# Seven block products for the down projections of two feed-forward blocks, with sums made by DMA

## The chip, the cores and the metric

The kernel runs on one core of one Trainium2 chip. The metric is device time in microseconds of one execution; the time before is the median of three runs.

## The reference

Three transformer-like blocks run one after the other on a sequence of 1024 tokens with 1024 features, all in float32. What matters here is the feed-forward part of each block, and in the second block a convolution:

```python
# first_block: D_FF = 4096 (called f1 in the kernel)
h = h + jnp.square(jax.nn.relu(hn @ w_up[layer])) @ w_down[layer]
...
# second_block: D_FF_2 = 2816 (f2), and a causal depthwise convolution of 31 taps on 256 channels
yc = causal_dwconv(yc, conv_w[l], conv_b[l])
...
hidden = jax.nn.silu(u[..., :D_FF_2]) * u[..., D_FF_2:]
x = x + jnp.einsum('bsf,fd->bsd', hidden, w_down[l])
...
# third_block: D_FF_3 = 4096 (f3)
f = jnp.square(jax.nn.relu(h @ w_fc1)) @ w_fc2
x = x + gate2 * rms_norm_3(f, norm2_post)
```

## The kernel before

Activations lie feature-major: a tile of 128 features by 1024 tokens, or by a half of 512. Every float32 operand of a big product is split into a rounded part and a remainder (`split`: ScalarE copies to the high part, L319, VectorE subtracts for the low part, L305), and every 128x128 by 128x512 product is three matmuls (`mm3`). So all weights, and all activations that return from DRAM, cost a 512 KB load, one ScalarE and one VectorE pass of 1024 columns.

`Stream` (`W`) is the list of all operands ("units") in the order of their use. A unit is loaded by the SyncE (SP) DMA queue into a `raw` buffer (two of them, four during a feed-forward block), and split into one of four slots of ring A, or two of ring B, as soon as one is free. `tick` is called after each group of matmuls and makes at most one split; `nd < ns + 2` keeps the loads at most two units ahead of the splits. `k.pe` counts the TensorE time of the matmuls written so far; it is a count made while the program is written, not a clock of the chip.

`up7` computes hidden = relu(x @ up)^2 with seven block products in place of eight (the pieces t1, t2, t3, t4 of the activations are made once; sums of weight halves are made by VectorE). It has groups of two units of 128 features: the first 8 (f1, f2) or 12 (f3) groups have one product computed ahead and reload it (`start`, a DMA of the GpSimd queue). Each hidden piece of 128x512 goes to DRAM (`gd`). `down7` reads them back, four units at a time, and makes the plain product with the down weights: for each 128x512 output tile, four units by three matmuls, and VectorE adds the tile to the residual in `X`. For f3 the last four units are done in parts of 512, 256 and 256 tokens, so that the last norm is short. `ada` units (weights of a small product, made by VectorE) are put between those of f1 and f2.

The residual of f1 and f2 is loaded into `X` by the GpSimd queue (`load_half`) before the first add. For f3 the residual is read back by the SP queue (`take_slots`, and one 2 MB load in `tail`).

In block 2 the convolution is spread over the first projections: VectorE does 18 of the 31 taps per channel block, ScalarE 12, GpSimd adds the ScalarE products into `cb` (`self.tt(cb, cb, s, ALU.add, nc.gpsimd)`).

Background work (norms, the convolution, the gated attention) is written as generators that `step` and `fine` advance between matmuls; each engine runs its instructions in the order in which they were written.

Of the kernel before, what the change touches and what calls it, by code (L numbers as in the profile page):

```python
# [8 lines left out]
F32 = mybir.dt.float32  # L9
# [47 lines left out]


def _feat(a):

    return np.ascontiguousarray(a.T.reshape(KT, P, a.shape[0]).transpose(1, 0, 2))


def lay_out(i):
# [16 lines left out]
    a["w1_up"] = _cols(i["w_up"][0])  # L81
    a["w1_down"] = i["w_down"][0].reshape(32, P, D)
    w = i["w_in_2"][0]
# [22 lines left out]
    a["w3_up"] = _cols(i["w_fc1_3"])  # L106
    a["w3_down"] = i["w_fc2_3"].reshape(32, P, D)

# [39 lines left out]
class Stream:  # L148
# [5 lines left out]
    def __init__(self, k):  # L154
        self.k = k
        self.seq = []
        self.nd = self.ns = 0
        self.free = {"A": 4, "B": 0}
        self.pools = {}
        self.bphase = ()  # L160
        self.raws = []
        self.groom = [False, False]

# [39 lines left out]
    def _split(self):  # L203
# [37 lines left out]
        self.ns += 1  # L241
        while self.nd < min(self.ns + 2, len(self.seq)):
            self.load()
        return True

    def tick(self):
        self.k.ada_flush()
        if self.ns < self.nd and self.k.pe - self.seq[self.ns].at > self.LEAD:
            self._split()
# [15 lines left out]
HALVES = ((0, 512), (512, 1024))  # L265


class Kern:
    def __init__(self, tc, a, out):
        self.tc, self.nc, self.a, self.out = tc, tc.nc, a, out  # L270
        self.bgs = []
        self.due = {}
        self.pe = 0.0
        self.clk = {tc.nc.vector: 0.0, tc.nc.scalar: 0.0, tc.nc.gpsimd: 0.0}
        self.stacks = []
        self.ada_pend = []
        self.adap = None


# [371 lines left out]

    CHUNKS = {"f1": [2, 2] + [4] * 7, "f2": [2] + [4] * 5, "f3": [2, 2] + [4] * 7}

# [4 lines left out]
    def setup(self):  # L658
# [46 lines left out]
        def ffn7(n, up, down, with_ada=0):  # L705
# [14 lines left out]
            for g in range(U):  # L720
# [3 lines left out]
                S[n + "g"].append(G)  # L724
            S[n + "h"], S[n + "d"] = [], []
            gd = S[n + "x"] = self.drp.tile([a[down].shape[0], P, T], F32, name="gd" + n)
            c = 0
# [167 lines left out]
    def up7(self, name):  # L895
# [10 lines left out]

        def relu2(dst, src, m, t, scale=1.0):
            self.act(dst, src, AF.Relu, scale=scale)
            self.act(dst, dst, AF.Square)
            nc.scalar.dma_start(out=gd[m, :, 512 * t:512 * t + 512], in_=dst)  # L910

# [11 lines left out]
        for g in range(0, M, 2):  # L923
# [7 lines left out]
            for i in (0, 1):  # L931
                u = first[g + i]
                self.part7(u, 512, H[1, 0], ps[i], False)
                W.done(u)
                s = scratch()
                if gated:
                    self.act(s, ps[i], AF.Copy)
                    nc.scalar.dma_start(out=cd[g + i], in_=s)
                else:
                    relu2(s, ps[i], 2 * (g + i), 0)  # L940
        self.wait(*self.norms.values())
# [6 lines left out]
        def slot():  # L948
            n[0] += 1
            return X1[:, (n[0] - 1) % 8]  # L950

# [5 lines left out]
        def start(g):  # L957

            ca = wide() if gated else None
            s1 = None  # L960
            if g < M:
                s1 = scratch() if gated else slot()
                nc.gpsimd.dma_start(out=s1, in_=sd[g])
                if gated:
                    nc.gpsimd.dma_start(out=ca[:, :512], in_=cd[g])
            return s1, ca

        if name == "f1":
            self.load_half(0)
        nxt = start(0)  # L970
        for g, G in enumerate(groups):
# [18 lines left out]
            if g >= M:  # L990
# [4 lines left out]
                else:  # L995
                    relu2(slot(), z, 2 * g, 0)
            x = self.ps()
# [10 lines left out]
            if not gated:  # L1008
                relu2(c22, c22, 2 * g + 1, 1)
            self.stt(c21, y, -1.0, w, ALU.mult, ALU.subtract)  # L1010
# [3 lines left out]
            else:  # L1014
                relu2(c21, c21, 2 * g + 1, 0)
            self.part7(W.get(d), 0, H[1, 1], x, False)
# [8 lines left out]
            else:  # L1025
                relu2(v, v, 2 * g, 1)
        W.groom[1] = True
        if name != "f3":
            for half in (0, 1)[name == "f1":]:
                self.load_half(half)  # L1030
        self.ext_es.close()
        self.open_ss()

    def load_half(self, half):
        c = half * 512
        for k in (0, 4):
            self.nc.gpsimd.dma_start(out=self.X[half][:, k:k + 4], in_=self.xd[:, k:k + 4, c:c + 512])

    def down7(self, name, add, tail, quarters=False):

        W = self.W
        D_, Gu = self.S[name + "d"], self.S[name + "h"]
        c = 0
        for j, n in enumerate(self.CHUNKS[name]):
# [9 lines left out]
            for part in self.PARTS if last and quarters else ((0, 0, 512), (1, 512, 1024)):  # L1054
                half, c0, c1 = part
                for m in range(KT):
# [12 lines left out]
                    while m == 0 and self.unsummed:  # L1069
                        self.fine(False, list(self.bgs))  # L1070
                    add(m, part, ps, first, last)
                    W.tick()
                    self.step()
# [27 lines left out]
    def add_ffn(self, a1, a2, g):  # L1101
        def add(m, part, ps, first, last):
            half, c0, c1 = part
            o = c0 - half * 512
            x = self.X[half][:, m, o:o + c1 - c0]
            self.tt(x, x, ps, ALU.add)
            if last:
# [44 lines left out]
    def block1(self):  # L1152
# [8 lines left out]
        dec = gp.tile([P, 2, 17], F32, name="dec")  # L1161
        lvl = gp.tile([P, 7, P], U8, name="lvl")
        g0, g0_es = self.pool("gate0", 1, None, "right")
        wg = g0.tile([NM, 256], F32, name="wg")
# [163 lines left out]
        for e in (gw_es, cp_es, tp_es, sg_es, gp_es):  # L1328
# [11 lines left out]
        self.up7("f1")  # L1340
        self.open_ring("f1d", ada=True)
        g = self.cols("norm_final_w")
        self.tt(self.g12, g, self.cols("ln1_g_2"), ALU.mult)
        a1, a2 = [], []
        self.down7("f1", self.add_ffn(a1, a2, g),
                 lambda part: self.norm2_gen(part, a1[part[0]], a2[part[0]], self.g12, None, g))
# [166 lines left out]
    def block2(self):  # L1513
# [18 lines left out]
        ca = [cp.tile([P, T], F32, name="ca%d" % m) for m in range(2)]  # L1532
        cb = cp.tile([P, T], F32, name="cb")

# [3 lines left out]

        NP = 12

        def conv():
            for m in range(2):
# [7 lines left out]
                self.ts(ca[m], yc[m][:, 0:T], w[0], self.col("conv_b_2", m), ALU.mult, ALU.add)  # L1550
                mul(1, cb)
                todo = list(range(2, 1 + NP))
                nd = 30 - NP
                for i, t in enumerate(range(1 + NP, 31)):
                    self.stt(ca[m], yc[m][:, t:t + T], w[t], ca[m], ALU.mult, ALU.add)
                    if todo and (NP - 1 - len(todo)) * nd <= i * (NP - 1):
# [7 lines left out]
                self.tt(ca[m], ca[m], cb, ALU.add)  # L1564
            for _ in range(5):
# [188 lines left out]


        self.up7("f2")
        self.open_ring("f2d", ada=True)
# [267 lines left out]
    def block3(self):  # L2025
# [203 lines left out]
        self.open_ring("f3d")  # L2229
        self.hp, e = self.pool("hp2", 1, None, "right")  # L2230
        self.ffn_es.insert(0, e)
        ac = []

        def add(m, part, ps, first, last):
            half, c0, c1 = part
            o = c0 - half * 512
            x = self.X[half][:, m, o:o + c1 - c0]
            if first:
                self.act(x, ps, AF.Copy)
            else:  # L2240
                self.tt(x, x, ps, ALU.add)
            if last:
                if m == 0 and o == 0:
                    ac.append(self.acc())
                if m == 0 and not xr:
                    take_slots()
                self.sq_add(ac[half], x, m, o)

        xr = []

        def take_slots():

            ts = []
            for q in "AB":
                while W.free[q] and len(ts) < 8:
                    W.free[q] -= 1
                    for n in ("hi", "lo"):
                        t = W.pools[q].tile([P, UW], F32R, tag=n, name="xr").bitcast(F32)[:, :T]
                        t = t.rearrange("p (a b) -> p a b", b=512)
                        k = len(ts)  # L2260
                        self.dma(t, self.xd[:, k:k + 2, 0:512])
                        ts.extend((t[:, 0], t[:, 1]))
            xr.append(ts)

        def tail(part):
            half, c0, c1 = part
            n, o = c1 - c0, c0 - half * 512
            self.unsummed = False
            if half and len(xr) < 2:
                t = self.hp.tile([P, KT, 512], F32, tag="h0", name="xr")  # L2270
                self.dma(t, self.xd[:, :, 512:])
                xr.append([t[:, k] for k in range(KT)])
            yield self.after(1.0)
# [6 lines left out]
            for k in range(KT + 1):  # L2280
# [3 lines left out]
                if k:  # L2284
                    f = self.X[half][:, k - 1, o:o + n]
                    x = xr[half][k - 1]
                    self.tt(f, f, x[:, o:o + n], ALU.add, gp if not half or k % 2 else None)
# [4 lines left out]
        self.down7("f3", add, tail, quarters=True)  # L2292

# [29 lines left out]
```

## Time and profile before

| what | us |
|---|---|
| median of 3 runs (3549.32 to 3553.84) | 3552.57 |
| the profiled execution, its own time | 3552.79 |
| its span, first to last instruction | 3550.7 |
| TensorE busy | 3421.8 |
| VectorE busy | 2258.7 |
| ScalarE busy | 1354.2 |
| GpSimd busy | 387.4 |

The mean granted TensorE clock is 0.978 of full speed. In the stages named here f1 lies at 500 to 1140 us of the span (down from 800), the convolution at 1230 to 1340, f2 at 1880 to 2520 (down from 2305), f3 at 2890 to 3534 (down from 3182).

### The profile page before, as it was taken

To read this page: it belongs to the slowest core of one execution; us is meant where nothing else is said; L and a number is where in the kernel's file an instruction comes from. 1 tells how busy PE (TensorE), PEld (TensorE's weight loads), DVE (VectorE), ACT (ScalarE), POOL (GpSimd) and SP (SyncE) were. 2 spreads that over 40 slices of the span, in tenths; PEclk is the share of its full clock that TensorE was granted. 3 is DMA by queue.
4 is the path that set the end of the run, shared out by engine and by line. 5 is a ranking of instruction groups with operands and counts; after the bars stand their busy time and mean duration, and the time that the engine had idled before them with its cause. 6 is when DMAs were issued, how large, how long until landed. Compare 5 with 4: busy or idle time off the path is not lost. (4 is left out here: it accounts for less than half of the span.)

```text
span 3550.7 us, 43690 instructions
## 1 busy us (share of the span) xinstructions
PE 3421.8 (96%) x16725; PEld 2813.7 (79%) x16725; DVE 2258.7 (64%) x3773; ACT 1354.2 (38%) x2018; POOL 387.4 (11%) x374
## 2 busy tenths in 40 slices
PE   7999999999999969999999999989999999999998
PEld 7788898888887757876698788778778878878887
DVE  5456376548665694567767988776665576645444
ACT  3432254442112442555634444421342564452111
POOL 0111020000001360000020000000132420000003
PEclk9999999999999979998999999999999999999999
DMA  3111444336443125445325322354222254443222
GB/s 106 48 43 48 151 138 165 115 117 207 145 137 101 62 82 172 133 123 153 85 105 165 122 84 85 108 206 140 89 76 63 82 182 149 134 163 119 95 83 72
DMA packets 176612, 413.07 MB, mean 116 GB/s; under 512 B 17832, under 2 KB 58488, under 8 KB 176276
## 3 DMA queue, kind: packets, MB, share of 16 engines
q1 hardware_dynamic: 133044, 325.34, 28.8%
q10 hardware_dynamic: 38304, 67.13, 5.1%
q0 software_dynamic: 5056, 17.83, 1.7%
q8 instruction: 131, 2.15, 0.3%
q14 instruction: 77, 0.63, 0.1%
HBM read 304.50 MB, written 105.63 MB: 116 GB/s over the span
## 5 line engine op out<-in xcount | busy, mean ns | idle before, releaser
L324 PE MATMUL mm<-Hh,whi 128*128 128x512 f32 (+3 forms) x3632 | 1384.7, 382 | 20.2 <-DVE X L305 12.0
L324 PE MATMUL mm<-Hl,whi 128*128 128x512 f32 (+3 forms) x3632 | 1370.2, 378 | 0.2
L324 PE MATMUL mm<-Hh,wlo 128*128 128x512 f32 (+3 forms) x3632 | 1366.1, 377 | 2.8 <-DVE wlo L305 2.8
L324 PEld LDWEIGHTS mm<-Hh,whi 128*128 128x128 f32 x3632 | 686.7, 189 | 162.1 <-DVE X L305 12.8
L324 PEld LDWEIGHTS mm<-Hh,wlo 128*128 128x128 f32 x3632 | 686.2, 189 | 136.0 <-DVE wlo L305 6.6
L324 PEld LDWEIGHTS mm<-Hl,whi 128*128 128x128 f32 x3632 | 686.9, 189 | 128.0 <-issue 1.2
L319 ACT ACTIVATE whi<-raw 128x1024 fp32r<-128x1024 f32 (+3 forms) x386 | 378.9, 992 | 711.2 <-PE mm L324 467.2
L305 DVE TENSOR_TENSOR wlo<-raw,whi 128x1024 fp32r<-128x1024 f32 (+3 forms) x386 | 451.2, 1176 | 178.9 <-ACT whi L319 166.3
L305 DVE TENSOR_TENSOR X<-X,mm 128x512 f32<-128x512 f32 (+1 forms) x478 | 312.2, 657 | 396.9 <-PE mm L324 389.8
L324 PE MATMUL mm<-t,whi 128*128 128x512 f32 x1296 | 408.6, 396 | 2.1 <-ACT whi L319 2.1
L324 PEld LDWEIGHTS mm<-t,whi 128*128 128x128 f32 x1296 | 243.0, 188 | 62.0 <-ACT whi L319 2.9
L324 PE MATMUL mm<-t,wlo 128*128 128x512 f32 x648 | 256.6, 396 | 2.2 <-DVE wlo L305 2.2
L319 ACT ACTIVATE Hh<-raw 128x1024 fp32r<-128x1024 f32 x86 | 89.3, 1057 | 381.5 <-PE mm L324 227.8
L321 ACT ACTIVATE X<-X 128x512 f32<-128x512 f32 (+1 forms) x226 | 151.9, 673 | 184.7 <-DVE X L310 152.8
L305 POOL TENSOR_TENSOR acc<-acc,sq 128x256 f32<-128x256 f32 (+1 forms) x108 | 116.2, 1077 | 912.2 <-ACT sq L321 836.9
L305 DVE TENSOR_TENSOR raw<-raw 128x512 f32<-128x512 f32 x216 | 145.2, 687 | 81.8 <-DMA raw<-in_w_up 79.8
L324 PEld LDWEIGHTS mm<-t,wlo 128*128 128x128 f32 x648 | 121.8, 188 | 33.5 <-DVE wlo L305 4.2
L305 DVE TENSOR_TENSOR Hl<-raw,Hh 128x1024 fp32r<-128x1024 f32 x86 | 104.5, 1221 | 45.6 <-ACT Hh L319 45.4
L324 PE MATMUL mm<-wlo,Hh 128*128 128x264 f32 (+4 forms) x336 | 111.5, 341 | 12.4 <-DVE wlo L305 12.4
L324 PE MATMUL mm<-whi,Hh 128*128 128x264 f32 (+4 forms) x336 | 112.0, 343 | 8.9 <-ACT whi L319 5.4
L310 DVE SCALAR_TENSOR_TENSOR ada<-raw,silc,ada 128x128 f32<-128x128 f32 x336 | 115.1, 350 | 7.9
L310 DVE SCALAR_TENSOR_TENSOR X<-mm,X 128x512 f32<-128x512 f32 x108 | 74.6, 690 | 60.3 <-PE mm L324 58.7
(290 smaller groups left out, 3467.8 us busy)
## 6 DMA issues: line engine op xcount, KB each, us to landing
raw<-in_w_up SPq DMA_DIRECT2D x136, 512.0 KB
raw<-gdf SPq DMA_DIRECT2D x86, 512.0 KB
raw<-in_w_down SPq DMA_DIRECT2D x86, 512.0 KB
gdf<-X ACTq DMA_DIRECT2D x108, 256.0 KB
raw<-in_w_ada SPq DMA_DIRECT2D x48, 512.0 KB
gdf<-X ACTq DMA_DIRECT2D x22, 512.0 KB
B<-qd SPq DMA_DIRECT2D x36, 256.0 KB
A<-qd SPq DMA_DIRECT2D x36, 256.0 KB
```

What stands on the lines that cost most here:

```text
L305: eng.tensor_tensor(out=out, in0=a, in1=b, op=op)
L310: self.nc.vector.scalar_tensor_tensor(out=out, in0=a, scalar=s, in1=b, op0=op0, op1=op1)
L319: self.nc.scalar.activation(out, in_, f, scale=scale, **kw)
L321: self.nc.scalar.activation(out, in_, f, bias=bias, scale=scale, **kw)
L324: self.nc.tensor.matmul(out, l, r, start=s, stop=e, skip_group_check=grp)
```

## The change

The down products of f1 and f3 are made in seven block products, each over all 16 pairs of hidden units: for the four quarters of a pair's weights (two units by two halves of the output features) and of its activations (two units by two halves of the tokens). Three products use a weight quarter as it is, four use a sum of quarters, called `sw`, which a list of DMAs makes in DRAM long before; the activation pieces are made by VectorE in `up7` and stored as seven pieces. Each product runs over eight e (two pairs each) with four PSUM tiles; both operands come through the stream, so each of the 56 steps of a down product needs two units of 512 KB. `sums` and `sums_step` issue 16 copies on the SP queue and 16 accumulating DMAs on the GpSimd queue for each of f1 and f3, one for each 12 us of `k.pe`: those of f1 in block 1, those of f3 from the start of f2's `up7`. `W.ahead` is 4 during the products.

For f1 all four residual loads are issued after `up7`. For f3 the residual is loaded into `Hh` by the GpSimd queue, and the last norm is one of 512 tokens. For f2 the first add becomes a ScalarE copy and the residual is added into `X` by four accumulating DMAs of 1 MB. In the convolution VectorE does 20 taps and ScalarE 10; the sums of the latter's products are made by accumulating DMAs of 512 KB in two tiles `cb`.

```diff
+def _quarters(w):
+    return np.ascontiguousarray(w.reshape(8, 2, 2, P, 2, 512).transpose(0, 2, 4, 3, 1, 5)).reshape(
+        8, 4, P, 2, 512)
...
-        while self.nd < min(self.ns + 2, len(self.seq)):
+        while self.nd < min(self.ns + self.ahead, len(self.seq)):
...
+    def sums(self, name, w):
+        S = self.S[name + "s"]
+        sync, pool = self.nc.sync, self.nc.gpsimd
+        for e in range(0, 8, 2):
+            r = slice(e, e + 2)
+            for i, q in ((0, 1), (2, 1), (1, 0), (3, 2)):
+                self.sums_todo.append((sync, S[i, r], w[r, q], {}))
+        for i, q in ((0, 3), (2, 0), (1, None), (3, None)):
+            for e in range(0, 8, 2):
+                r = slice(e, e + 2)
+                src = w[r, q] if q is not None else S[0 if i == 1 else 1, r]
+                self.sums_todo.append((pool, S[i, r], src, dict(accum_op=ALU.add, max_dma_last_dim=4096)))
+
+    def sums_step(self, pace=12.0):
+        if self.sums_todo and self.pe >= self.sums_at:
+            eng, dst, src, kw = self.sums_todo.pop(0)
+            eng.dma_start(out=dst, in_=src, **kw)
+            self.sums_at = self.pe + pace
...
+    ORDER = ("P1", "P2", "P6", "P7", "P4", "P5", "P3")
...
+                sw = S[n + "s"] = self.drp.tile([4, 8, P, 2, 512], F32, name="sw" + n)
+                A = {"P1": a[down][:, 0], "P2": a[down][:, 2], "P4": a[down][:, 3],
+                     "P5": sw[0], "P6": sw[1], "P7": sw[2], "P3": sw[3]}
+                for i in self.ORDER:
+                    for e in range(8):
+                        S[n + "d"].append([W.add(x[e].rearrange("p a b -> p (a b)"), D, n + "d")
+                                           for x in (A[i], gd[PIECE[i]])])
...
 (up7, at the end of each group, not for f2)
-                relu2(v, v, 2 * g, 1)
+                relu2(v, v)
+                t1_, t2_, t4_ = slot(), slot(), slot()
+                self.tt(t1_, ca, v, ALU.subtract)
+                self.tt(v, c22, v, ALU.subtract)
+                self.stt(t2_, t1_, -1.0, c22, ALU.mult, ALU.subtract)
+                self.stt(t4_, t2_, -1.0, c21, ALU.mult, ALU.subtract)
+                for i, t in ((3, t1_), (5, v), (4, t2_), (6, t4_)):
+                    nc.gpsimd.dma_start(out=piece(i, g), in_=t)
...
+    def down_parts(self, name, out, tail):
+        W.ahead = 4
+        new = True
+        for n, i in enumerate(self.ORDER):
+            if n == 6:
+                self.drop_raws()
+                W.ahead = 2
+            if new:
+                ps = [self.ps() for _ in range(4)]
+            for e in range(8):
+                wa, wb = (W.get(u) for u in D_[8 * n + e])
+                for m in range(4):
+                    for k in (0, 1):
+                        w, x = slice(k * 512 + m * P, k * 512 + m * P + P), slice(k * 512, k * 512 + 512)
+                        self.mm3(ps[m], wa.hi[:, w], wa.lo[:, w], wb.hi[:, x], wb.lo[:, x],
+                                 new and e == 0 and k == 0, e == 7 and k == 1, not new)
+                    if e == 7:
+                        z = ps[m]
+                        if i == "P1":
+                            self.act(s[:, m], z, AF.Copy)
+                        elif i == "P2":
+                            out(0, m, z, 1)
...
+            new = i not in ("P1", "P6", "P5")
...
 (down7, now for f2 alone)
+                    if residual and n == 4 and m % 4 == 3:
+                        s = slice(m - 3, m + 1)
+                        self.nc.gpsimd.dma_start(out=self.X[half][:, s], in_=self.xd[:, s, c0:c1],
+                                                 accum_op=ALU.add)
...
 (block 2, the convolution)
-        NP = 12
+        NP = 10
...
-                        self.tt(cb, cb, s, ALU.add, nc.gpsimd)
+                        nc.gpsimd.dma_start(out=cb[len(todo) % 2], in_=s, accum_op=ALU.add)
```

## Rows read from the trace of the kernel before

**Rows 1.** The page: busy us of the engines, share of the span, instructions.

```profile
PE 3421.8 (96%) x16725; PEld 2813.7 (79%) x16725; DVE 2258.7 (64%) x3773; ACT 1354.2 (38%) x2018; POOL 387.4 (11%) x374
```

**Rows 2.** Windows: stretch, length, busy us and instructions by engine, clock, DMA share, GB/s.

```profile
560.00:630.00 70.00, 70.00 (x302) 56.42 (x302) 45.15 (x62) 32.38 (x46) 1.63 (x3) 1.00 0.45 146
...
1230.00:1340.00 110.00, 76.36 (x344) 66.43 (x343) 109.49 (x70) 46.75 (x52) 69.09 (x22) 0.83 0.24 78
...
1935.00:2090.00 155.00, 150.73 (x642) 119.65 (x641) 142.37 (x166) 66.48 (x68) 4.31 (x8) 1.00 0.34 114
...
2315.00:2320.00 5.00, 0.78 (x2) 0.68 (x3) 3.54 (x7) 0.00 (x0) 0.00 (x0) 0.50 1.02 407
...
3250.00:3300.00 50.00, 50.00 (x217) 40.51 (x216) 21.38 (x26) 8.15 (x8) 0.00 (x0) 1.00 0.26 85
...
3534.00:3550.70 16.70, 2.82 (x16) 2.20 (x15) 11.34 (x31) 0.62 (x2) 6.89 (x9) 0.64 0.38 126
```

**Rows 3.** The page's costliest groups: count, busy us, mean ns, idle before.

```profile
L305 DVE TENSOR_TENSOR wlo<-raw,whi 128x1024 fp32r<-128x1024 f32 (+3 forms) x386 | 451.2, 1176 | 178.9 <-ACT whi L319 166.3
...
L305 DVE TENSOR_TENSOR raw<-raw 128x512 f32<-128x512 f32 x216 | 145.2, 687 | 81.8 <-DMA raw<-in_w_up 79.8
```

**Rows 4.** One tile, the convolution's tap sums: duration ns min/median/max, first and last start.

```profile
L310 DVE SCALAR_TENSOR_TENSOR ca<-yc,smalls,ca x36: 1150/1285/3508, 1229.6 to 1338.1; 128x1024 f32<-128x1024 f32 x36
```

**Rows 5.** Lines from 1130 to 1360 us: count, busy us, mean ns, idle before.

```profile
L310 DVE SCALAR_TENSOR_TENSOR ca<-yc,smalls,ca 128x1024 f32<-128x1024 f32 x36 | 78.0, 2174 | 0.4
```

**Rows 6.** Waits from 2300 to 2345 us: total us, times, longest.

```profile
PE mm L324 <- DVE X L305: 12.0, 1, 12.0
```

**Rows 7.** The page's DMA queues: packets, MB, share of 16 engines' span.

```profile
q1 hardware_dynamic: 133044, 325.34, 28.8%
...
q0 software_dynamic: 5056, 17.83, 1.7%
```

**Rows 8.** All DMAs issued by GpSimd: count, KB each, median us from issue to landing.

```profile
X<-xd POOLq DMA_DIRECT2D x8, 1024.0 KB, 7.1
...
X<-sdf POOLq DMA_DIRECT2D x20, 256.0 KB, 3.1
...
X<-cdf POOLq DMA_DIRECT2D x8, 256.0 KB, 3.0
st<-sdf POOLq DMA_DIRECT2D x8, 256.0 KB, 3.1
```

**Rows 9.** DMA view from 1481.5 to 1483.4 us: all packets, and two 8-row transfers.

```profile
DMA packets 32, 0.01 MB, mean 4 GB/s; under 512 B 16, under 2 KB 32, under 8 KB 32
...
B<-mh SPq DMA_DIRECT2D x1, 4.0 KB
B<-ml SPq DMA_DIRECT2D x1, 4.0 KB
```

**Rows 10.** Timeline of SP and ACT at the start of f3's down product.

```profile
3165.28 0.60 SPq L328 DMA_DIRECT2D xr<-xd  x1
3167.95 4.82 SPq L183 DMA_DIRECT2D raw<-in_w_down  x2
...
3181.22 1.06 ACT L319 ACTIVATE whi<-raw 128x1024 fp32r<-128x1024 f32 x1 [6.02 <-DMA raw<-in_w_down]
...
3189.35 2.83 SPq L183 DMA_DIRECT2D raw<-in_w_down  x2
...
3192.83 1.06 ACT L319 ACTIVATE whi<-raw 128x1024 fp32r<-128x1024 f32 x1 [0.61 <-DMA raw<-in_w_down]
```

**Rows 11.** Timeline: a weight load and its first matmul in f1; two spills in block 1.

```profile
593.73 0.33 SPq L183 DMA_DIRECT2D raw<-in_w_up  x1
...
608.97 0.63 PE L324 MATMUL mm<-t,whi 128*128 128x512 f32 x2
...
242.37 0.33 SPq L328 DMA_DIRECT2D yc<-sh  x1
...
248.65 0.32 SPq L328 DMA_DIRECT2D yc<-sh  x1
```

More of the change, by code (lines that the diff above doesn't have):

```diff
@@ L161, in __init__ @@
         self.raws = []
+        self.ahead = 2
         self.groom = [False, False]
@@ L1027, in up7 @@
         W.groom[1] = True
-        if name != "f3":
-            for half in (0, 1)[name == "f1":]:
-                self.load_half(half)
         self.ext_es.close()
         self.open_ss()
[L1034 to L1037, printed above, removed]
+    def down_parts(self, name, out, tail):
+        W = self.W
+        D_ = self.S[name + "d"]
+        sp, e = self.pool("sums", 1, None, "right")
+        self.ffn_es.insert(0, e)
+        s = sp.tile([P, 4, 512], F32, name="s_")
+        v = sp.tile([P, 4, 512], F32, name="v_")
+        W.ahead = 4
[13 more added lines that the diff above has]
+                                 new and e == 0 and k == 0, e == 7 and k == 1, not new)
+                    if m == 3:
+                        W.done(wa)
+                        W.done(wb)
+                    if e == 7:
[4 more added lines that the diff above has]
+                            out(0, m, z, 1)
+                        elif i == "P6":
+                            self.tt(v[:, m], z, s[:, m], ALU.add)
+                        elif i == "P7":
+                            self.tt(s[:, m], z, s[:, m], ALU.add)
+                        elif i == "P4":
+                            out(0, 4 + m, z, -1, s[:, m])
+                        elif i == "P5":
+                            out(1, 4 + m, z, -1, s[:, m])
+                        else:
+                            out(1, m, z, 1, v[:, m])
+                    W.tick()
+                    if m % 2:
+                        self.step()
+                    else:
+                        self.fine()
+            new = i not in ("P1", "P6", "P5")
+            if i == "P4":
+                self.unsummed = True
+                self.norms[0] = self.bg(tail((0, 0, 512)))
+            elif i == "P3":
+                self.unsummed = True
+                self.norms[1] = self.bg(tail((1, 512, 1024)))
@@ L1105, in add @@
             x = self.X[half][:, m, o:o + c1 - c0]
-            self.tt(x, x, ps, ALU.add)
+            if first:
+                self.act(x, ps, AF.Copy)
+            else:
+                self.tt(x, x, ps, ALU.add)
             if last:
@@ L1162, in block1 @@
         lvl = gp.tile([P, 7, P], U8, name="lvl")
+        self.sums("f1", a["w1_down"])
+        self.sums_at = 60.0
         g0, g0_es = self.pool("gate0", 1, None, "right")
@@ L1341, in block1 @@
         self.open_ring("f1d", ada=True)
+        for half in (0, 1):
+            for k in (0, 4):
+                nc.gpsimd.dma_start(out=self.X[half][:, k:k + 4],
+                                    in_=self.xd[:, k:k + 4, half * 512:half * 512 + 512])
         g = self.cols("norm_final_w")
@@ L1344, in block1, with out @@
         a1, a2 = [], []
-        self.down7("f1", self.add_ffn(a1, a2, g),
+        got = [0, 0]
+        def out(half, m, z, sign, extra=None):
+            x = self.X[half][:, m]
+            op = ALU.add if sign > 0 else ALU.subtract
+            if extra is not None:
+                self.tt(x, x, extra, op)
+            self.tt(x, x, z, op)
+            while half and self.unsummed:
+                self.fine(False, list(self.bgs))
+            if not got[half]:
+                a1.append(self.acc())
+                a2.append(self.acc())
+            self.sq_add(a1[half], x, got[half])
+            self.sq_add(a2[half], x, got[half], 0, g[:, m:m + 1], self.nc.vector)
+            got[half] += 1
+        self.down_parts("f1", out,
                  lambda part: self.norm2_gen(part, a1[part[0]], a2[part[0]], self.g12, None, g))
@@ L1563, in conv @@
                 yield
-                self.tt(ca[m], ca[m], cb, ALU.add)
+                for s in cb:
+                    self.tt(ca[m], ca[m], s, ALU.add)
             for _ in range(5):
@@ L2229, in block3, with out @@
         self.open_ring("f3d")
-        self.hp, e = self.pool("hp2", 1, None, "right")
-        self.ffn_es.insert(0, e)
+        xr = self.Hh.bitcast(F32)
+        for k in (0, 4):
+            nc.gpsimd.dma_start(out=xr[:, k:k + 4, :T], in_=self.xd[:, k:k + 4])
         ac = []
[L2234 to L2239, printed above, removed]
-            else:
[L2241 to L2263, printed above, removed]
+        got = [0, 0]
+        def out(half, m, z, sign, extra=None):
+            x = self.X[half][:, m]
+            if extra is None:
+                self.act(x, z, AF.Copy)
+            elif sign > 0:
+                self.tt(x, z, extra, ALU.add)
+            else:
+                self.stt(x, z, -1.0, extra, ALU.mult, ALU.subtract)
+            if not got[half]:
+                ac.append(self.acc())
+            self.sq_add(ac[half], x, got[half])
+            got[half] += 1
         def tail(part):
@@ L2290, in tail @@
             self.free(pb)
-        self.down7("f3", add, tail, quarters=True)
+        self.down_parts("f3", out, tail)
     def run(self):
```

60 lines of the change are left out of this document (36 added, 24 removed).

## The prediction

> **What bounds the kernel now.** I read the page first, then windows of 50 us and less, then waits, timeline and DMA views of the places that the diff touches. TensorE is busy 3421.8 us of the span [rows 1], and in the long product stages without a gap: 217 matmuls of 512 columns in 50 us at full clock, 0.2304 us each, and the windows from `up7` (560 to 630 us in f1, 1935 to 2090 us in f2) show how close VectorE comes to it [rows 2]. So a product that needs fewer matmuls saves their time, as long as operands arrive. Outside these stages two places lose TensorE time: the convolution (33.6 of 110 us, VectorE busy without a pause) and the start of f2's down product (12.0 us) [rows 2, 6].
>
> **The change part by part.** I sum gains and costs against the profiled execution, 3552.8 us, which is 0.2 us over the median; a change under 0.2% (7 us) is what a measurement of this kernel can't tell from none.
>
> *Matmuls.* A down product has 8 output tiles by 2 halves by 32 units by 3 = 1536 matmuls now, and 7 products by 4 tiles by 16 blocks by 3 = 1344 then. 192 fewer by 0.2304 us is 44.2 us, for two blocks **-88.5 us**.
>
> *Operands of the products.* 112 units in place of 64 are loaded and split; a VectorE pass is 1.18 us [rows 3]. A step e is 24 matmuls, 5.53 us, and needs two of them: 2.4 us of VectorE beside 5.5 of TensorE, 1 MB in 5.5 us (190 GB/s, against 407 reached in one window [rows 2]). All of it lies beside matmuls, with two steps split ahead in six slots. Uncovered are the ends of products with two adds and two squares per tile in f1 (P4, P5): some 2 us each. I take **+4 us**, between 0 and 20 (16 steps late by one such pass).
>
> *Four more VectorE operations per group of `up7`.* 20 groups with a reload are the tight ones: five parts of 12 matmuls, 13.8 us. VectorE is busy 45.15 of 70 us there, 8.9 us of a group, and gets 4 by 0.687 us more: 11.7 of 13.8, 84% [rows 2, 3]. The nearest row is f2's own `up7`: at 142.4 of 155 us (92%) TensorE loses 4.3 us [rows 2]. 20 groups are 276 us, so 0 to 8; I take **+4**. The eight (f1) and four (f3) groups without a reload have more room.
>
> *f2's first add.* TensorE waits 12.0 us for VectorE's add into `X` at the start [rows 6], which stands behind 4 MB of residual loads. A ScalarE copy takes its place and the loads are gone; the copy still stands behind a split that waits for the last hidden piece. Between 0 and 12; I take **-9**. The accumulating loads come 30 us before their next use; a plain 1 MB by GpSimd lands in 7.1 us, 256 KB in 3.1 [rows 8], and twice the first is still covered.
>
> *Convolution.* The 36 tap operations last 1150 ns undisturbed and up to 3508 ns while GpSimd adds, 78.0 us in all [rows 4, 5]. 40 taps at 1150 ns, without the GpSimd adds, are 46 us. VectorE is full for these 110 us and TensorE lacks 33.6; about 30 us of VectorE go. Against it: ScalarE must wait for a 512 KB accumulating DMA before it can reuse `cs`: between 4.4 us (between the two plain rows of [rows 8]) and twice that, two at a time, for eight per channel block. I take **-25**, between -34 and +10. The Trainium skill, SBUF — State Buffer, "Who interferes with whom", says that a VectorE instruction with two SBUF inputs and a GpSimd instruction that reads SBUF block each other; the taps' 1150 and 3508 ns agree.
>
> *End.* From the last big matmul to the end are 16.7 us with a part of 256 tokens [rows 2]; one of 512 doubles the eight scale-and-add steps of some 0.7 us, but the norm before it leaves the stage: **+3**, between 0 and 6. Residual loads of 4 MB by GpSimd beside the first steps of f1 and f3: **+2**, between -3 (f3's load leaves the SP queue) and 10.
>
> These sum to -88.5 + 4 + 4 - 9 - 25 + 3 + 2 = **-109.5 us**.
>
> *The copies of the weight quarters.* This is the part that decides. Each of the 16 is 1 MB from DRAM to DRAM in two blocks (`r` is two e's; source quarters are not contiguous with each other), on the SP queue, on which every weight comes. How many of the 16 DMA engines does such a transfer use? GpSimd's 44 DMAs, all of 128 rows [rows 8], left 5056 packets: 17.83 MB in packets of 4 KB are 4352, and 704 more, 16 for each [rows 7]. In the stretch with two 8-row transfers there are 32 packets: 16 of 512 B of data, and 16 small ones, 8 for each [rows 9]. So one small packet per engine, and a transfer of 8 rows uses 8 engines. By that, one of two blocks uses two. The Trainium skill states it so (DMA: Bandwidth & Descriptors, "Why a DMA increments its semaphore by 16 and not by 1"): the number of engines is the largest up to 16 that divides the slowest dimension of both sides. The 8 packets agree; no run here shows a two-block copy.
>
> An engine moves 24.9 GB/s in the fullest window (407 GB/s at 1.02 of 16), 19.9 by the SP queue's mean [rows 2, 7]. 512 KB on each of two engines are 21 us, at most 26. They are issued one per 12 us of `k.pe`, and a tick comes every part, so in `up7` one per five parts, 13.8 us. The queue can't keep up. What stands behind is every weight load: each spreads over all engines and lands when its share on these two has. The trace shows what a bulk transfer on the queue does: a weight load issued 2.7 us after the 2 MB `xr` was split 13.3 us after its issue, an undisturbed pair within 3.5 [rows 10].
>
> In f2's `up7`: 16 by 21.1 are 338 us of those two engines, and some 32 loads add 1.3 us each (their 32 KB): 380 us. The matmuls written between the first copy and the last take 15 by 13.8 = 208 us, and a load is issued 15 us ahead of its first matmul (593.73 to 608.97, [rows 11]). 380 - 208 - 15 = 157; I take **+150**, between 100 (a look-ahead of four slots) and 235 (at 26 us).
>
> In block 1 matmuls of the attention lie between, so a copy comes every 15 us or so, and the look-ahead is longer, four units of 14 us. But the convolution's spills go by SP too, and the second split into `sh` (one buffer) must wait for the first spill: issued at 242.37, the next at 248.65 [rows 11]. From about 82 us on (an estimate: `sums_at` is 60 of `k.pe`, which starts with the first matmul and runs some per cent behind the span) eleven or twelve copies are issued before it, 240 us of engine time and 20 of loads, which end at 340: ScalarE, and with it TensorE, waits some 90 us. **+90**, between 30 and 140.
>
> Accumulating DMAs on the GpSimd queue follow later, not in the SP queue's order; I cost them at nothing, since f1's sums are needed 300 us after, f3's 800. If an accumulate of 1 MB took over 14 us in a row, f2's residual adds would stand behind them.
>
> Together -109.5 + 240 = +130.5: **3683 us**.
>
> **Rivals.** *The copies spread over all engines* (the other side): then one takes 64 KB per engine, under 3 us, every 13.8, and hides like the residual loads. 3553 - 109.5 = 3443 us. For it speaks that no two-block copy is in the trace; against it the 8 packets. It decides from about 15 us per copy: below that the queue keeps up. *Two engines, but the loads are mostly covered*, because slots and raws hold more than I count: a loss of 0 to 60, some 3480. Against it: 16 times 7 us are missing in each stage whatever the look-ahead. *The accumulating DMAs are slow too* and hold the GpSimd queue, f2's residual adds and the convolution's ScalarE: 40 to 100 us on top, some 3760. *VectorE becomes the bound of `up7`* in f1 and f3: +20, within the range of each case.
>
> **How the numbers follow.** Chances: forecast 0.68, spread copies 0.20, covered loads 0.06, slow accumulates 0.06. The likeliest is 3683, its own range 3590 to 3780 (block 1 at 30 and f2 at 110, or 120 and 220). The range that leaves out no more than 2 in 10 reaches half into the spread case: 3440 to 3780. Faster are the spread copies and the covered loads, 0.20 + 0.06, slower the forecast and the slow accumulates, 0.68 + 0.06; 0.01 of each I move to a loss that just cancels the gains: faster 0.25, slower 0.73, same 0.02.
>
> **What would show it.** In the profile after: about 200 us more of TensorE idle in block 1 (80 to 400) and from 1900 on (in old time), with ScalarE or VectorE waiting for raw from the weights and a granted clock at its lower level; the down stages of f1 and f3 at 310 us without gaps; the tap operations near 1150 ns; the start of f2's down product without the 12 us. If there are no waits for weights in block 1, the copies were spread and the time is near 3443. Wrong would also be a convolution in which ScalarE waits for its DMAs, or `up7` of f1 and f3 with gaps.

## The result, and the profile after

The changed kernel takes 3952.51 us (median of 4 runs, 3949.45 to 3956.68) against 3551.8 us: the ratio is 1.1129, with a 95% interval of 1.111 to 1.1149. The forecast was 3683, range 3440 to 3780. The sign was right; the loss is 401 us where 130 were forecast.

The page after, in the order of [rows 1, 7]: busy time of the engines, then the DMA queues.

```profile
PE 3440.4 (87%) x16245; PEld 2802.0 (71%) x16245; DVE 2262.2 (57%) x3745; ACT 1440.1 (36%) x2105; POOL 459.8 (12%) x540
...
q1 hardware_dynamic: 144164, 405.04, 30.9%
q0 software_dynamic: 58656, 103.01, 10.8%
```

TensorE has 480 instructions fewer than in [rows 1] and yet is busy 19 us longer: the clock has fallen where it waits. The windows show where (columns as in [rows 2]).

```profile
100.00:150.00 50.00, 31.62 (x140) 26.80 (x139) 18.45 (x23) 18.87 (x28) 7.35 (x10) 0.75 0.30 86
...
450.00:500.00 50.00, 22.90 (x100) 19.79 (x99) 9.43 (x12) 4.66 (x6) 3.73 (x3) 0.73 0.52 137
...
900.00:950.00 50.00, 16.85 (x60) 13.00 (x60) 11.48 (x16) 6.31 (x9) 3.67 (x4) 0.64 0.48 141
...
1700.00:1810.00 110.00, 94.12 (x425) 80.29 (x426) 76.57 (x88) 46.07 (x57) 11.13 (x13) 0.92 0.66 170
2390.00:2545.00 155.00, 151.49 (x647) 121.11 (x647) 141.62 (x165) 66.51 (x69) 3.77 (x7) 1.00 0.32 111
3700.00:3750.00 50.00, 50.00 (x216) 40.31 (x215) 23.70 (x23) 21.11 (x24) 4.33 (x3) 1.00 0.59 189
3928.40:3949.70 21.30, 5.42 (x26) 4.66 (x24) 9.82 (x19) 1.28 (x3) 7.95 (x6) 0.56 0.27 99
```

The first three (block 1, f1's `up7`) have a third to two thirds of their time empty, and the clock granted is 0.64 to 0.75, between its two levels of 1.2 and 2.4 GHz; f2's `up7` (2390 to 2545) is as full as in [rows 2], and f3's down product (3700) runs without a gap. So the loss is ahead of f1's down product, and none of it where the prediction put the larger half, in f2's `up7`. The view of the tile of the sums says why (duration in ns, then first and last start):

```profile
L683 SPq DMA_DIRECT2D swf<-in_w_down x32: 582/594/982, 22.8 to 1148.1; - x32
L683 POOL DMA_DIRECT2D swf<-in_w_down x16: 1888/1966/2697, 76.4 to 1126.5; - x16
L683 POOL DMA_DIRECT2D swf<-swf x16: 881/916/982, 186.9 to 1204.2; - x16
```

All 64 transfers, f3's too, have been issued by 1204 us. The code writes f3's at the start of f2's `up7` (after the attention, which ends at 2208 us here). But the builder that makes the engines' instruction streams does not keep the written order for instructions that depend on nothing, as these do: f3's 32 ran from 591 us on, nearly all in f1's `up7`. So what is said ahead of the prediction, that each engine runs its instructions in the order in which they were written, does not hold for them. A stretch of the timeline there (start, length, engine, in brackets the idle time before and its cause):

```profile
904.14 1.97 POOL L683 DMA_DIRECT2D swf<-in_w_down  x1 [0.70 <-DMA X<-gdf]
...
910.82 0.81 SPq L191 DMA_DIRECT2D raw<-in_w_up  x2
911.68 0.59 SPq L683 DMA_DIRECT2D swf<-in_w_down  x1
...
951.27 1.15 POOL L1086 DMA_DIRECT2D gdf<-X  x2 [42.83 <-DMA swf<-in_w_down]
952.07 1.42 DVE L318 TENSOR_TENSOR X<-X,X 128x512 f32<-128x512 f32 x2 [26.64 <-DMA swf<-in_w_down]
...
954.73 2.62 DVE L318 TENSOR_TENSOR raw<-raw 128x512 f32<-128x512 f32 x4
956.24 2.52 ACT L332 ACTIVATE whi<-raw 128x1024 fp32r<-128x1024 f32 x3 [29.49 <-DVE raw L318]
960.32 0.82 SPq L191 DMA_DIRECT2D raw<-in_w_up  x2
```

Two weight loads are issued at 910.82, and their first use is at 954.73, 44 us later ([rows 10]: 3.5 us undisturbed). Copies and accumulates are in flight meanwhile, and both have a part in it. The SP queue's packets from 930.55 to 949.7 us are those of a copy alone, 14 of 64 KB:

```profile
q1 hardware_dynamic: 14, 0.92, 11.0%
```

So both loads had landed some 20 us after their issue, behind the copy before them. For the rest VectorE, which has to add the weight halves, stands 26.64 us at the activation pieces, and GpSimd 42.83 us at a store, by the profile both until an accumulate ends. The waits from 700 to 1240 us sum it up (total us, times, longest): VectorE waits 35.4 us for weights that it has to add, and 53.0 in two waits for an accumulate and for a store of a piece. The list of issues by GpSimd (count, KB, median us to landing) shows what an accumulate takes, against 7.1 us for a plain 1 MB in [rows 8]:

```profile
PE mm L337 <- ACT whi L332: 153.2, 16, 32.6
...
ACT whi L332 <- DVE raw L318: 92.7, 10, 29.5
POOL gdf L1086 <- DMA swf<-in_w_down: 80.2, 3, 42.8
...
DVE raw L318 <- DMA raw<-in_w_up: 35.4, 4, 27.4
...
DVE X L318 <- DMA swf<-in_w_down: 26.6, 1, 26.6
DVE X L323 <- DMA gdf<-X: 26.4, 1, 26.4
```

```profile
swf<-in_w_down POOLq DMA_DIRECT2D x16, 1024.0 KB, 52.3
swf<-swf POOLq DMA_DIRECT2D x16, 1024.0 KB, 24.9
...
X<-xd POOLq DMA_DIRECT2D x8, 1024.0 KB, 12.1
...
cb<-cs POOLq DMA_DIRECT2D x16, 512.0 KB, 6.7
```

The span cut at the same matmuls in every profile (first and last matmul that reads a piece `t` in each `up7`, first with block 2's and block 3's token-major products, first of the attention's outputs), in us; the last five columns are kernels of the experiments below:

| stretch | before | after | no sums | two-block, tied | copies two-block, tied | rows, tied | rows, f3's later |
|---|---|---|---|---|---|---|---|
| block 1 to f1's `up7` pieces | 533.0 | 833.4 | 533.2 | 806.1 | 757.8 | 537.4 | 539.5 |
| f1 `up7` | 271.1 | 447.0 | 278.5 | 283.6 | 285.2 | 283.4 | 286.1 |
| f1 down, to block 2 | 433.3 | 414.8 | 412.1 | 408.1 | 409.1 | 410.2 | 410.3 |
| convolution, to attention | 203.3 | 186.5 | 186.9 | 188.6 | 185.9 | 186.1 | 185.4 |
| attention, to f2's pieces | 469.5 | 468.6 | 467.8 | 504.3 | 496.7 | 467.6 | 468.5 |
| f2 `up7` | 388.2 | 387.1 | 387.9 | 592.4 | 564.7 | 421.1 | 387.2 |
| f2 down, to block 3 | 277.0 | 267.1 | 267.5 | 293.5 | 263.9 | 271.1 | 271.9 |
| block 3, to f3's pieces | 341.1 | 341.2 | 341.3 | 341.4 | 341.0 | 339.4 | 338.4 |
| f3 `up7` | 248.4 | 264.0 | 264.3 | 264.4 | 267.9 | 264.8 | 265.8 |
| f3 down and end | 385.8 | 340.1 | 338.5 | 339.3 | 341.2 | 340.2 | 340.3 |

After less before: +300 in block 1 and the start of f1's `up7`, +176 in f1's `up7` from its pieces on, and all the rest together -77.

### The profile page after: what moved, and what is told of

Read it like the earlier page. It is cut to its first block, busy times and chain, and to the rows that moved or that the text cites. A ratio compares the mean times of both kernels' runs of the same rounds, so it can differ in the third digit from the quotient of the medians.

```text
span 3949.7 us, 43380 instructions
## 1 busy us (share of the span) xinstructions
PE 3440.4 (87%) x16245; PEld 2802.0 (71%) x16245; DVE 2262.2 (57%) x3745; ACT 1440.1 (36%) x2105; POOL 459.8 (12%) x540
## 3 DMA queue, kind: packets, MB, share of 16 engines
q0 software_dynamic: 58656, 103.01, 10.8%
## 5 line engine op out<-in xcount | busy, mean ns | idle before, releaser
L337 PE MATMUL mm<-Hh,whi 128*128 128x512 f32 (+3 forms) x2576 | 985.9, 384 | 195.4 <-ACT whi L332 70.1
L337 PE MATMUL mm<-Hh,wlo 128*128 128x512 f32 (+3 forms) x2576 | 971.9, 378 | 17.1 <-DVE wlo L318 16.9
L337 PE MATMUL mm<-Hl,whi 128*128 128x512 f32 (+3 forms) x2576 | 974.1, 378 | 0.3 <-DVE Hl L318 0.2
L318 DVE TENSOR_TENSOR wlo<-raw,whi 128x1024 fp32r<-128x1024 f32 (+3 forms) x546 | 642.1, 1192 | 486.5 <-ACT whi L332 475.7
L337 PEld LDWEIGHTS mm<-Hh,whi 128*128 128x128 f32 x2576 | 498.0, 193 | 299.4 <-ACT whi L332 73.9
L337 PEld LDWEIGHTS mm<-Hh,wlo 128*128 128x128 f32 x2576 | 496.7, 193 | 112.8 <-DVE wlo L318 24.6
L337 PEld LDWEIGHTS mm<-Hl,whi 128*128 128x128 f32 x2576 | 497.6, 193 | 87.0 <-issue 1.4
L337 PE MATMUL mm<-whi 128*128 128x512 f32 x896 | 359.5, 402 | 11.3 <-DVE mod L318 5.7
L337 PE MATMUL mm<-wlo,whi 128*128 128x512 f32 x896 | 356.7, 398 | 1.5 <-DVE wlo L318 1.5
L337 PE MATMUL mm<-whi,wlo 128*128 128x512 f32 x896 | 355.3, 397 | 0.0
## 6 DMA issues: line engine op xcount, KB each, us to landing
swf<-in_w_down POOLq DMA_DIRECT2D x16, 1024.0 KB, 52.3
```

Source lines behind the costliest of these rows:

```text
L318: eng.tensor_tensor(out=out, in0=a, in1=b, op=op)
L337: self.nc.tensor.matmul(out, l, r, start=s, stop=e, skip_group_check=grp)
```

## The experiments

**1. The form of the transfers, as the builder places them.** Each transfer is written over the 128 rows in place of the two blocks: both kinds, the copies alone, the accumulates alone; and a kernel without sums.

```diff
+    def rows(v):
+        return v.rearrange("e p a b -> p e (a b)")
...
-    self.sums_todo.append((sync, S[i, r], w[r, q], {}))
+    self.sums_todo.append((sync, rows(S[i, r]), rows(w[r, q]), {}))
-    self.sums_todo.append((pool, S[i, r], src, dict(...)))
+    self.sums_todo.append((pool, rows(S[i, r]), rows(src), dict(...)))
```

> All 64 transfers of the sums are written row by row (128 rows of two 4 KB pieces in place of two blocks), the same bytes. Theory A (a two-block transfer, copy or accumulate, runs on two DMA engines; 32 copies of 19.4 us and 16 accumulates from the weights of some 42 us are 1290 us of these two engines, and all weight loads wait for them): the whole loss before the end of f1's up7 goes, 3445 us, 3425 to 3480. Theory B (the recorded one: only the copies in the weight queue cost): the same 3443. Theory C (the accumulating itself or its traffic, whatever the form, holds the GpSimd queue and the engines): over 3600.

> Only the 32 copies are written row by row; the accumulates stay as they are. Theory A: 16 accumulates of 42 us on two engines are 672 us of some 800, interleaved with the loads packet by packet, so that most is hidden: 3450 to 3600. Theory B: 3443. Theory C: over 3800.

> Only the accumulates are written row by row; the 32 copies stay in two blocks. Theory A: 621 us of two engines are left of 1290, in the weight queue: 3600 to 3750. Theory B: no change, about 3950. Theory C: about 3950 too, less only what the copies were not to blame for.

For the kernel without sums the edit takes both calls of `sums` out and reads quarters in their place:

```diff
-    "P5": sw[0], "P6": sw[1], "P7": sw[2], "P3": sw[3]
+    "P5": a[down][:, 1], "P6": a[down][:, 1], "P7": a[down][:, 0], "P3": a[down][:, 2]
```

> Leaves out: the sums are not made; the four products read plain quarters of the weights in place of them. All else is as in the changed kernel. All theories: 3443 (3553 less 109.5), and this prices the rest of the change; the difference to the row-by-row version is what well spread sums cost, 0 to 15 us.

Measured: both in rows 3628.39 us (ratio 1.0214, 1.0199 to 1.023); copies in rows 3795.34 and accumulates in rows 4021.98 (one run each); without sums 3480.79 (0.9801, 0.9782 to 0.9821). Theory C alone allows 3628 (it said over 3600), none gave 3795 or 4022, and all had 3443 for the kernel without sums. The windows of "both in rows":

```profile
100.00:150.00 50.00, 15.21 (x56) 12.31 (x57) 4.61 (x6) 4.20 (x8) 9.10 (x10) 0.57 1.04 250
250.00:300.00 50.00, 14.63 (x72) 10.69 (x68) 5.26 (x11) 2.83 (x3) 6.86 (x6) 0.66 1.03 222
350.00:400.00 50.00, 49.17 (x358) 43.14 (x357) 34.98 (x68) 16.34 (x24) 9.21 (x13) 1.00 0.15 48
```

With the other form the builder placed them otherwise, all 64 transfers in the first 312 us: all DMA engines are full there (1.04), weights wait, and after that this kernel runs like the one without sums. So the runs with another form changed place and form at once, and none of the three can be read as the price of a form, nor as a proof of theory C. What stands is the kernel without sums: the sums cost 472 us of 3952, and the rest of the change brings 71.

**2. The same forms, tied to their places.** Each transfer is put behind the last instruction written before it on its queue, an order alone with no wait, so that f1's stand in block 1 and f3's from f2's `up7` on, as the code has it.

```diff
-            eng.dma_start(out=dst, in_=src, **kw)
+            last = next(i for i in reversed(self.nc.cur_bb.bb.instructions)
+                        if i.engine == (mybir.EngineType.SP if eng is self.nc.sync else mybir.EngineType.Pool))
+            with self.tc.issue_after(last):
+                eng.dma_start(out=dst, in_=src, **kw)
```

> All sums transfers row by row, and each is tied behind the last instruction written before it on its queue, so that f1's stand in block 1 and f1's up7 and f3's in f2's up7 and after, one by one, as the code paces them. Theory A (two DMA engines per two-block transfer, and the place in the program): the sums cost next to nothing any more, 3490 us, 3475 to 3520. Theory C (accumulating in DRAM costs by itself, wherever it stands): over 3550.

> The changed kernel's two-block transfers, but tied to the places where the code writes them (f3's in f2's up7, not in f1's). This is what the recorded prediction assumed: its +240 on the 3481 of the run without sums is 3720; with the accumulates on two engines too, 3720 to 3850. Theory P (place alone made the loss): near 3500.

> Tied to their places; copies row by row, the accumulates from the weights in two blocks. Theory A: the accumulates are 336 us of two engines per block, off the weight queue's order: 3490 to 3560. Theory C: over 3600.

> Tied to their places; copies in two blocks, accumulates row by row. The recorded working (copies at two engines, +90 in block 1 and +150 in f2's up7): 3720, 3600 to 3800. Theory P (place alone): near 3500.

Measured: both in rows 3521.21 (0.9915, 0.9895 to 0.9934), both in two blocks 4023.47, accumulates alone in two blocks 3656.59, copies alone in two blocks 3915.28 (the last three one run each). Theory P is refuted: in its written place the two-block form costs even 71 us more than after, and more than the 3850 that I gave at most. Two-block copies cost 3915 - 3521 = 394 us, two-block accumulates 135 alone and 108 beside two-block copies. The first is over the 3800 that I gave for it at most, and the second over 3560, on the side of theory C; but the version in rows, 29 us under C's bound, refutes it: the accumulating itself does not cost that. In the list of issues the accumulate from the weights falls from 54.2 us (accumulates in two blocks) to 14.3 (both in rows):

```profile
swf<-in_w_down POOLq DMA_DIRECT2D x16, 1024.0 KB, 54.2
swf<-swf POOLq DMA_DIRECT2D x16, 1024.0 KB, 34.3
```

```profile
swf<-in_w_down POOLq DMA_DIRECT2D x16, 1024.0 KB, 14.3
swf<-swf POOLq DMA_DIRECT2D x16, 1024.0 KB, 22.3
```

These medians hold the time that one accumulate stands behind others of its queue. The first of f1's, issued at 326 us in both kernels with none before it in its queue, shows the form alone, in two blocks and then in rows:

```profile
swf<-in_w_down POOLq DMA_DIRECT2D x1, 1024.0 KB, 49.8
```

```profile
swf<-in_w_down POOLq DMA_DIRECT2D x1, 1024.0 KB, 8.8
```

That a two-block copy uses two engines is now seen itself. In the kernel with two-block copies, from 222 to 232 us, one pair of packets of 64 KB starts and a copy ends:

```profile
DMA packets 4, 0.13 MB, mean 13 GB/s; under 512 B 2, under 2 KB 2, under 8 KB 2
```

Two small packets close it, one per engine as [rows 9] had it. The trace has 512 packets of 64 KB for the 32 copies, two at a time, 2.42 us each: 16 per copy, eight in a row on each of two engines, 19.4 us.

**3. Four blocks.** As the tied kernel with two-block copies, but each copy is 2 MB in four blocks, and there are half as many at twice the distance.

```diff
-                self.sums_todo.append((sync, S[i, r], w[r, q], {}))
+                if e % 4 == 0:
+                    t = slice(e, e + 4)
+                    self.sums_todo.append((sync, S[i, t], w[t, q], {}))
...
-            self.sums_at = self.pe + pace
+            self.sums_at = self.pe + (2 * pace if eng is self.nc.sync else pace)
```

> As the tied version with two-block copies and row-by-row accumulates (3915 us), but each copy is 2 MB in four blocks and there are half as many at twice the distance: the same bytes, four DMA engines in place of two, 19.4 us per transfer against 24 of the code's count. If the loss comes from two engines that can't keep up: most of the 394 us over the version all in rows goes, 3530 to 3640. If it falls with the share of the engines alone: half, some 3720. If copies in the weight queue cost by themselves: 3850 to 3950.

Measured: 3713.01 us (one run). From 237 to 257.5 us one such copy ends, with four small packets:

```profile
DMA packets 18, 0.81 MB, mean 40 GB/s; under 512 B 4, under 2 KB 4, under 8 KB 4
```

A copy again lasts some 20 us, and the queue now keeps up (one per 24 of `k.pe`; in f2's `up7` they start 32 to 64 us apart). Still 192 us over the version in rows are lost: 12.0 us for each of 16 copies. With two blocks it was 394 / 32 = 12.3 us for each of 32. Engines times us are the same in both (32 x 2, 16 x 4), so, as far as two single runs tell it (number and distance changed together), the loss goes by the number of copies of this length, not by the engines they hold (my second reading gave the right time for a wrong reason) and not by a queue that falls behind. One holds the loads behind it for some 20 us, whether 2 or 4 engines are late: here a load issued at 2109.1 us has moved 96 of its 128 packets of 4 KB by 2113, and the other 32 only from 2129 to 2133, when the copy has ended. The 8 us between 20 and 12 are not simply what the look-ahead covers, since the 12 hold more than waits for weights. In f2's `up7` TensorE is busy 417 of 566 us with two-block copies at a granted clock of 0.86, and 384 of 387 at 1.00 in the version of experiment 4: about a fifth of that loss is matmuls at the lower clock. One wait of 28 us there is for VectorE, which stands at a reload on GpSimd's queue.

**4. What the sums still cost in rows.** f3's begin after f2's `up7` in place of before.

```diff
-        self.sums("f3", a["w3_down"])
         self.up7("f2")
+        self.sums("f3", a["w3_down"])
```

> The row-by-row, tied version, but with f3's sums begun after f2's up7 in place of before it. There the tied version lost 33 us of its 40 over the run without sums (f2's up7 421 us in place of 388). If f3's transfers cross f2's own reloads and stores there: 3490, 3480 to 3505. If the sums cost the same wherever they stand: 3521.

Measured: 3496.41 us (0.9836, 0.9821 to 0.985). f2's `up7` is back at 387.2 us. This version is 58 us faster than the kernel before, and so faster than both kernels of the change. It is 16 us from the kernel without sums.

**5. The rest of the change, term by term**, each from the version of 4: without the four VectorE operations of a group (f1, f3), with the convolution of before, with part of the piece operations on GpSimd, and without most of the VectorE work of the `ada` units.

```diff
-                t1_, t2_, t4_ = slot(), slot(), slot()
-                self.tt(t1_, ca, v, ALU.subtract)
-                self.tt(v, c22, v, ALU.subtract)
-                self.stt(t2_, t1_, -1.0, c22, ALU.mult, ALU.subtract)
-                self.stt(t4_, t2_, -1.0, c21, ALU.mult, ALU.subtract)
+                t1_, t2_, t4_ = ca, c22, c21
```

> As the version with f3's sums later, but leaves out the four VectorE operations per group that make the activation pieces (the stores stay, of other data). If these operations are what f1's and f3's up7 lost 7 and 16 us to: 20 us less than that version, 12 to 25, some 3470. If the doubled stores or loads did it: 0 to 5 less.

```diff
-        NP = 10
+        NP = 12
...
-                        nc.gpsimd.dma_start(out=cb[len(todo) % 2], in_=s, accum_op=ALU.add)
+                        self.tt(cb, cb, s, ALU.add, nc.gpsimd)
```

> As the version with f3's sums later, with the convolution as in the kernel before (18 taps on VectorE, the sums by GpSimd adds). If the convolution's part brought what its stage shows (203.3 to 186.9 us): 16 us more, 10 to 25; by the recorded 25: 25 more. If the stage gained by something else: 0 to 5 more.

```diff
-                self.tt(v, c22, v, ALU.subtract)
-                self.stt(t4_, t2_, -1.0, c21, ALU.mult, ALU.subtract)
+                self.tt(v, c22, v, ALU.subtract, nc.gpsimd)
+                self.tt(t4_, t1_, c21, ALU.subtract, nc.gpsimd)
+                self.tt(t4_, t4_, c22, ALU.add, nc.gpsimd)
```

> As the version with f3's sums later, with two of the four piece operations made on GpSimd (three adds there). If VectorE's order holds up TensorE in up7: 5 to 12 us less. If GpSimd's adds slow VectorE's operations on the shared memory, as in the convolution: 0 to 20 more.

```diff
             else:
-                self.stt(acc, w, self.silc[:, k:k + 1], acc, ALU.mult, ALU.add)
+                pass
```

> As the version with f3's sums later (3496 us), but leaves out seven of the eight VectorE operations of each ada unit, in f1's and f2's down products (their loads and matmuls stay). If that work holds up f1's product: f1's stage 10 to 20 us shorter, 3480. If loads or the residual do it: 0 to 5.

Measured: without the piece operations 3476.83 (0.9781, 0.9765 to 0.9798), 20 us less, of which the two `up7` have 8.1 and 11.9: they are the cost. Convolution undone 3509.69 (0.9874, 0.9859 to 0.9888), 13 us more, so its part brings 13. With adds on GpSimd 3546.45 (0.9976, 0.9964 to 0.9987), 50 us more: the second theory, and worse than its bound. Lines of f3's `up7`, GpSimd variant first (3000 to 3180 us), then version 4 (2950 to 3130 us):

```profile
L318 POOL TENSOR_TENSOR X<-X,X 128x512 f32<-128x512 f32 x17 | 26.3, 1554 | 73.5 <-DVE X L318 73.4
...
L323 DVE SCALAR_TENSOR_TENSOR X<-X,X 128x512 f32<-128x512 f32 x7 | 9.9, 1410 | 0.1
...
L318 DVE TENSOR_TENSOR raw<-raw 128x512 f32<-128x512 f32 x40 | 39.2, 996 | 23.7 <-DMA raw<-in_w_up 23.6
```

```profile
L323 DVE SCALAR_TENSOR_TENSOR X<-X,X 128x512 f32<-128x512 f32 x12 | 8.2, 686 | 0.1
...
L318 DVE TENSOR_TENSOR raw<-raw 128x512 f32<-128x512 f32 x44 | 28.8, 687 | 20.3 <-DMA raw<-in_w_up 20.1
```

VectorE's piece operation beside GpSimd's adds takes 1410 ns on average in place of 686, and its sums of weight halves, of which some stand beside an add, 996 in place of 687.

Without most of the `ada` work 3456.52 (0.9736, 0.972 to 0.9753), 40 us less; f1's down stretch is 379.5 in place of 410.3 us, more than the 10 to 20 us that I had expected. Its windows there, without `ada` work first, then version 4:

```profile
870.00:970.00 100.00, 100.00 (x440) 80.92 (x439) 57.25 (x70) 42.54 (x46) 4.58 (x3) 1.00 0.76 253
```

```profile
880.00:980.00 100.00, 96.36 (x408) 77.00 (x407) 69.65 (x121) 39.66 (x41) 4.19 (x3) 0.97 0.68 231
```

VectorE is at 70% and TensorE loses 3.6 of 100 us; at 57% it loses none, with more bytes moved in the same time. So it was not the loads.

## Why the prediction was right and wrong, by its steps

*Two engines per copy, some 21 us*: right, 19.4 us. The number of engines by the count of small packets held, for four blocks too, and so did the rule of the Trainium skill (DMA: Bandwidth & Descriptors, "Why a DMA increments its semaphore by 16 and not by 1"): 2 and 4 small packets.

*The price of the copies, +240*: the step that failed most. I let the queue overrun its pace and took a look-ahead of 15 us off once, 7.5 us per copy. In place it is 394 us, 12.3 us per copy (220 in block 1 against 90; 172 in f2, 29 of them ahead of its pieces, against 150; both against the version in rows). Experiment 3 shows that the model itself was wrong and not only its size: the sentence "it decides from about 15 us per copy: below that the queue keeps up" put four blocks (9.7 us per MB) at no loss, and they lost 192 us. In block 1 I ended the sum at the second spill, 340 us; with copies tied in place they ran on to 608 us. And TensorE's clock, which I left out there, is granted at 0.53 to 0.88 in each 50 us from 350 to 650 us of that kernel, with gaps of TensorE in each.

*Accumulates "at nothing"*: wrong, 108 to 135 us. They too are in two blocks where they read the weights (52.3 us each, 14.3 in rows), and I had asked that question of the copies alone. The rival that had them slow gave 40 to 100 us, and a condition of 14 us in a row: with none before it, one takes 49.8 us in two blocks, and 8.8 in rows. These prices are those of the tied kernels, in which f1's `up7` loses hardly anything to the sums (283 to 285 us against 278.5 without them). How the 176 us that the changed kernel lost there divide between copies and accumulates no run shows.

*Where f3's transfers run*: wrong. "Those of f3 from the start of f2's `up7`" holds for the code, not for the streams; they crossed f1's `up7`. It changed where the loss lies, and made it 71 us smaller than in the written place (3952 against 4023), so it is not what made the kernel slow.

*The rest, -109.5*: measured -71. f2's first add, -9: 277.0 to 267.5 us, right. f3's down product and the end, -44 + 3 and a part of the +2: 385.8 to 338.5, -47, right. The convolution, -25: -13 by undoing it, 16 by its stretch. The taps are at 1150 to 1287 ns, but with a median of 1278 where I took 1150 (some 5 us for the 40), and ScalarE then waits 32.6 us for its accumulating DMAs from 1695 to 1810 us, the cost I named against it. Operations in `up7`, +4 with bounds 0 and 8: 20 us by leaving them out, which is the price of the rival that has VectorE as the bound of `up7`. My bound came from f2, with VectorE at 92% and hardly a loss; a mean busy share doesn't tell where in a group the operations stand. Operands of the products, +4 with bounds 0 and 20: f3's are free, but f1's down stretch gained 21 us in place of 44 less some 2, and the last run puts it on the `ada` work on VectorE, which is as before but now stands beside two splits per step. TensorE's gaps in this stretch are 5 us before, 22 without sums and none without most of the `ada` work.

*What decided it*: the two-block form of the transfers. From the kernel without sums, 3481, the runs add 40 us for sums in rows, 394 for two-block copies and 108 for two-block accumulates beside them, and take off 71 for the place: 3952. No rival's time came true, but the mechanisms of two did, slow accumulates (108 to 135 us) and VectorE in `up7` (20 us). The spread copies (3443) would need the other form, the place and the two mis-sized terms right: the best version reached 3496.

## What to carry to other kernels

Write a DRAM-to-DRAM transfer over its 128 rows, not over a short outer dimension, and ask the same of each accumulate; then look in the trace for how many packets run at once. Here each copy of 20 us on 2 or 4 of the engines that the weight stream uses cost the kernel about 12 us, even where the queue had time to spare. Work that depends on nothing stands where the builder puts it: check the order in the trace before pricing it, and tie it where its place matters.

## What had not been expected of the hardware

An accumulate of 1 MB from DRAM to DRAM over rows landed in 8.8 us when none stood before it, close to the 7.1 us of a plain 1 MB load before the change; in two blocks it took 49.8 us. The medians of whole kernels, 9.5 to 32.2 us over rows, hold the time in line behind others. For the same data, the software queue carries 58656 packets with two-block accumulates and 29984 with rows (103.01 and 102.78 MB); the 28672 more are packets of 8 bytes. And beside GpSimd's adds VectorE's operations with both inputs in SBUF took twice as long in `up7` (686 to 1410 ns), while 13 with one input in PSUM that ran beside an add kept 679 ns on average. So moving two of VectorE's four extra operations to GpSimd made the kernel 50 us slower.
